# A sliding-window copy: the last staged batch shifted by one block and stored from 128 partitions, and fewer direct rows sent in halves

## Chip, core and metric

The kernel runs on one core of a Trainium2 chip. The metric is device time in microseconds (us), the median of several executions. The program does nothing but copy, so everything below is about the 16 DMA engines of the core, about HBM, the large memory of the chip, and about SBUF, the memory inside the core (128 rows, called partitions).

Two things about the numbers. First, times of one kernel on one chip agree within 1 per cent, mostly within 0.4, in four sets of experiments, each set on one chip. Here they are called chips A, B, C and D. (The chips of the very first runs, before and changed, are not on record.) Kernels are compared within one set only. Each chip was used in one set, so a lasting property of the chip and its condition at that hour (what else used its memory, for example, which is not on record) cannot be told apart; "chip" below means both. Second, all runs were of the fast state: every granted clock on record is 1.0.

## The reference

`x` has shape (32, 4096, 256), float32. Windows of 64 rows start every 32 rows; there are 127 in each of the 32 batches.

```python
for i in range(127):
    result[:, i] = x[:, 32 * i : 32 * i + 64].copy()
```

A *block* is 32 rows, 32 KB. A batch has 128 blocks. Window `w` is blocks `w` and `w + 1`: all blocks but the first and the last of a batch are written twice. The output is 266 MB.

## The kernel before

There are two ways to fill the output.

- **Direct**: HBM to HBM. One window (64 KB) is read and written, as two packets of 32 KB. A byte of output costs a byte of HBM reads and one pass through a DMA engine.
- **Staged**: a batch is loaded once into SBUF (128 partitions, one block each) and stored twice, as first halves and as second halves of the windows. It spares half of the reads, but three passes through the engines serve two bytes of output. Packets are 16 KB.

Eleven of the 32 batches are staged. Three of the core's engines issue the transfers: SP the direct windows (DMA queue q1), ACT the loads and stores (q10), and POOL the edge windows that are left over (q0), at the end. All three queues share the 16 engines. A direct transfer of 16 windows gives each engine two packets and one small completion packet. The same 16 windows "in halves" are two transfers, so each engine gets two packets and *two* completion packets. The kernel before uses that to set the balance of the queues.

```python
    def windows(self, q, b, w0, n, half=None, piece=DIRECT, count=None):
        size = 2 * blk if half is None else blk
        off = blk if half else 0
        # ... one DMA: n rows of `size`, x to out, step 2 * blk in out and blk in x

# Staging.store, the last staged batch (batch 30)
        if g == len(self.batches) - 1:
            for half, p0, rows in ((0, 0, 112), (0, 112, 15), (1, 1, 15), (1, 16, 112)):
                self.c.count_last(self.c.store(q, self.tiles[i], self.batches[g], half, p0, rows))
            return
        for half in (0, 1):    # all others: 128 partitions, one row too many each time
            self.c.store(q, self.tiles[i], self.batches[g], half).then_inc(self.stored[i], 16)

# the direct batches, seven groups of 16 windows each
    per, loads, stores = 6, 6 * 17, 34
                at = turns % (loads + per * stores)
                share += 9 if at < loads else 3      # twelfths: 3/4 in loads, 1/4 in stores
                if share >= 12:
                    share -= 12; turns += 4
                    c.windows(ring_d, b, first(b) + 16 * j, 16, 0)
                    c.windows(ring_d, b, first(b) + 16 * j, 16, 1, ...)
                else:
                    turns += 3
                    c.windows(ring_d, b, first(b) + 16 * j, 16, ...)
# ... the edge windows
        ring_r = nc.gpsimd
        ring_r.wait_ge(near, 16)                     # q1 is nearly done
        for i, b in enumerate(...):
            for g in waits[b]:
                st.wait_stored(ring_r, g)            # a staged store spilled one row here
            for w, n in rest_parts(b):
                c.windows(ring_r, b, w, n, None, PIECES[i % 1], count_soft)
```

A store of 128 rows for 127 windows writes one wrong row into a neighbouring batch. The edge windows there are copied after that store and put it right. The last staged batch, 30, has no such cover, so it is stored as 112 and 15 rows.

## Time and profile before

| | before |
|---|---|
| median time (first three runs) | 752.06 us |
| span of the profiled execution | 743.5 us |
| bytes through the engines | 313.16 MB |

These lines are from the profile page of the kernel before: the span; the DMA row (busy share of the engines in 40 slices, 9 is 90 per cent or more); the rate in the same slices; the queues with packets, MB and share of the engines' time.

```profile
span 743.5 us, 321 instructions
DMA  8999999999999999999999999999999999999995
GB/s 368 431 430 427 426 436 436 423 440 420 431 432 425 427 438 420 435 427 421 439 423 408 431 434 432 434 424 433 427 437 429 430 425 437 421 435 432 414 420 191
q1 hardware_dynamic: 8080, 154.15, 48.5%
q10 hardware_dynamic: 9002, 138.35, 43.8%
q0 software_dynamic: 1008, 20.65, 6.8%
```

The engines are busy from the second slice to the last but one. The kernel can get faster only by moving fewer bytes, by quicker packets, or by a better end.

The windows view shows stretches: start and end in us, length, POOL's busy time with instructions, tensor clock, busy share of the DMA engines, GB/s.

```profile
20.00:140.00 120.00, 0.00 (x0) 1.00 1.00 429
140.00:400.00 260.00, 0.00 (x0) 1.00 1.01 428
700.00:720.00 20.00, 0.00 (x0) 1.00 0.98 415
720.00:735.00 15.00, 0.00 (x0) 1.00 0.98 362
735.00:743.50 8.50, 0.00 (x0) 1.00 0.05 19
```

The rate is level until the end. From 720 us on, the engines are busy but slower. In the DMA view of 725 to 735 us (queues as above), hardly anything but edge windows is left:

```profile
q0 software_dynamic: 161, 3.24, 87.5%
q10 hardware_dynamic: 12, 0.11, 3.3%
```

In the packet records of the trace, a 16 KB packet takes 0.611 us and a 32 KB packet 1.213 us when nothing hinders it (these are the medians before). The **excess** is the time that packets take above this, summed and divided by 16 engines: microseconds of span lost to slow packets.

### The profile page before, as it was taken

Reading aid. Unit: us, or ns where it says so; the run is one execution under the profiler, and the core shown is the slowest. Engines: PE = TensorE matmul, PEld = TensorE weight load, DVE = VectorE, ACT = ScalarE, POOL = GpSimd, SP = SyncE. Lnnn points to the kernel's source line nnn. Section 1 sums busy time; section 2 is a strip of 40 time slices with the busy share of each in tenths; the row PEclk is TensorE's granted clock in tenths of the full one; section 3 lists DMA queues with packets and bytes.
Section 4 is the critical chain, followed back from the end, with each engine's and each line's share of the span. In section 5 each row is a group of like instructions: output and inputs, shape, how many; then the busy total and the mean of one; then the engine's idle time right before and its main releaser. Section 6 shows DMA issues by size and latency. Waiting matters only on the chain.

```text
span 743.5 us, 321 instructions
## 1 busy us (share of the span) xinstructions
POOL 12.4 (2%) x25
## 2 busy tenths in 40 slices
POOL 0000000000000000000000000000000000050000
DMA  8999999999999999999999999999999999999995
GB/s 368 431 430 427 426 436 436 423 440 420 431 432 425 427 438 420 435 427 421 439 423 408 431 434 432 434 424 433 427 437 429 430 425 437 421 435 432 414 420 191
DMA packets 18092, 313.16 MB, mean 421 GB/s; under 512 B 4312, under 2 KB 4312, under 8 KB 4312
## 3 DMA queue, kind: packets, MB, share of 16 engines
q1 hardware_dynamic: 8080, 154.15, 48.5%
q10 hardware_dynamic: 9002, 138.35, 43.8%
q0 software_dynamic: 1008, 20.65, 6.8%
q14 instruction: 2, 0.02, 0.0%
HBM read 220.92 MB, written 266.99 MB: 656 GB/s over the span
## 4 chain that ended last, share of the span: by engine, by line
another core or an unknown queue 91%; POOL 2%; issue 0%; POOLq 0%; SPq 0%
POOL out_dram L48 2%; POOLq L226 0%; SPq L165 0%; POOLq L107 0%
## 5 line engine op out<-in xcount | busy, mean ns | idle before, releaser
L48 POOL DMA_DIRECT2D out_dram<-in_x_dram x21 | 12.2, 584 | 674.3 <-DMA out_dram<-in_x_dram 651.4
L212 POOL MEMSET const-float32-0.0<- 128x1 f32 x1 | 0.1, 93 | 0.2 <-issue 0.2
L212 POOL MEMSET const-bfloat16-1.0<- 128x1 bf16 x1 | 0.1, 97 | 0.0
L212 POOL MEMSET const-uint8-127<- 128x1 uint8 x1 | 0.1, 93 | 0.0
L212 POOL MEMSET const-float32-1.0<- 128x1 f32 x1 | 0.1, 92 | 0.0
## 6 DMA issues: line engine op xcount, KB each, us to landing
out_dram<-in_x_dram SPq DMA_DIRECT2D x83, 1024.0 KB, 97.1
out_dram<-xb ACTq DMA_DIRECT2D x20, 4096.0 KB, 137.8
out_dram<-in_x_dram SPq DMA_DIRECT2D x128, 512.0 KB, 90.5
xb<-in_x_dram ACTq DMA_DIRECT2D x11, 4096.0 KB, 122.1
out_dram<-in_x_dram POOLq DMA_DIRECT2D x21, 960.0 KB, 46.5
out_dram<-xb ACTq DMA_DIRECT2D x2, 3584.0 KB, 127.3
out_dram<-xb ACTq DMA_DIRECT2D x2, 480.0 KB, 112.8
```

The costliest lines, as they stand in the source:

```text
L48: q.dma_start(out=self.oap((b * self.nw + w0) * 2 * blk + off, [[2 * blk, n], [1, size]]), in_=bass.AP(self.x.tensor, self.x.offset + (b * ...
L212: nc = _bacc.Bacc("TRN2", target_bir_lowering=False, num_devices=1)
```

## The change

Two parts with one intent: a better balanced end. Batch 31 is staged in place of 30, loaded from one block earlier, so that both its stores have 128 partitions. Their first rows fall into the last two windows of batch 30 and are wrong there. A small transfer, the *repair*, rewrites these two windows after the last staged store. And fewer rows go in halves: a half in load phases (before: three quarters), a sixth in store phases (before: a quarter).

```diff
-    staged = [*range(1, B - 3, 3), B - 2]
+    staged = [*range(1, B, 3)]
...
+    st = Staging(c, tc, pool, x.dtype, staged, 6, {B - 1})    # {B - 1}: shifted by 1
...
-            out=t[:, :], in_=self.xap(b * self.nb, [[self.blk, self.nb], [1, self.blk]]),
+            in_=self.xap(b * self.nb - shift, [[self.blk, self.nb], [1, self.blk]]),
...
-        w = b * self.nw + p0 - half
+        w = b * self.nw - half - shift
...
-            for half, p0, rows in ((0, 0, 112), (0, 112, 15), (1, 1, 15), (1, 16, 112)):
-                self.c.count_last(self.c.store(q, self.tiles[i], self.batches[g], half, p0, rows))
-            return
...
-                share += 9 if at < loads else 3
+                share += 6 if turns % (loads + per * stores) < loads else 2
...
+                if todo == 7:      # the one row of batch 31 that the shift leaves out
+                    count(c.windows(ring_d, B - 1, c.nw - 1, 1, 1, 2048), done)
...
+        st.wait_stored(ring_r, len(staged) - 1)
+        ap = [[c.blk // 4, 8], [c.blk, 2], [1, c.blk // 4]]
+        oap = [[c.blk // 4, 8], [2 * c.blk, 2], [1, c.blk // 4]]
+        count(                     # the repair
+            ring_r.dma_start(
+                out=c.oap((last * c.nw + c.nw - 2) * 2, oap), in_=c.xap(last * c.nb + c.nw - 2, ap)
+            ),
+            rest,
+        )
```

The cut leaves out bookkeeping: semaphores, and a slightly different order of the edge windows.

More of the change, by code (lines that the diff above doesn't have):

```diff
@@ L9, with __init__ @@
 DIRECT, IN, OUT = 32768, 16384, 16384
-PIECES = (32768,)
 class Copier:
-    def __init__(self, nc, tc, x, out, B, L, D, W, S, n_win):
+    def __init__(self, x, out, B, L, D, W, S, n_win):
         assert W == 2 * S and L % S == 0
-        self.nc, self.tc, self.x, self.out = nc, tc, x, out
+        self.x, self.out = x, out
         self.B = B
@@ L22, in __init__ @@
         self.nw = n_win
-        self.total = 0
-        self.done = tc.alloc_semaphore("done")
-        self.last = tc.alloc_semaphore("last")
-        self.last_total = 0
     def xap(self, block, dims):
         return bass.AP(self.x.tensor, self.x.offset + block * self.blk, dims)
-    def oap(self, elem, dims):
-        return bass.AP(self.out.tensor, self.out.offset + elem, dims)
-    def count(self, dma):
-        dma.then_inc(self.done, 16)
-        self.total += 16
-    def count_last(self, dma):
-        dma.then_inc(self.last, 16)
-        self.last_total += 16
@@ L42, in windows, with oap @@
-    def windows(self, q, b, w0, n, half=None, piece=DIRECT, count=None):
-        blk = self.blk
-        size = 2 * blk if half is None else blk
-        off = blk if half else 0
-        (count or self.count)(
-            q.dma_start(
-                out=self.oap((b * self.nw + w0) * 2 * blk + off, [[2 * blk, n], [1, size]]),
-                in_=bass.AP(
-                    self.x.tensor,
-                    self.x.offset + (b * self.nb + w0) * blk + off,
-                    [[blk, n], [1, size]],
-                ),
-                max_dma_last_dim=piece,
-            )
+    def oap(self, half_window, dims):
+        return bass.AP(self.out.tensor, self.out.offset + half_window * self.blk, dims)
@@ L57, in windows, with load @@
+    def windows(self, q, b, w0, n, half=None, piece=DIRECT):
+        blk = self.blk
+        row = [1, 2 * blk if half is None else blk]
+        h = half or 0
+        return q.dma_start(
+            out=self.oap((b * self.nw + w0) * 2 + h, [[2 * blk, n], row]),
+            in_=self.xap(b * self.nb + w0 + h, [[blk, n], row]),
+            max_dma_last_dim=piece,
         )
-    def load(self, q, t, b):
+    def load(self, q, t, b, shift):
         return q.dma_start(
-            out=t[:, :], in_=self.xap(b * self.nb, [[self.blk, self.nb], [1, self.blk]]),
+            out=t[:, :],
+            in_=self.xap(b * self.nb - shift, [[self.blk, self.nb], [1, self.blk]]),
@@ L62, in load, with store @@
             max_dma_last_dim=IN,
         )
-    def store(self, q, t, b, half, p0=0, n=None):
-        blk = self.blk
-        n = self.nb if n is None else n
-        w = b * self.nw + p0 - half
+    def store(self, q, t, b, half, shift):
+        w = b * self.nw - half - shift
         return q.dma_start(
-            out=self.oap(w * 2 * blk + half * blk, [[2 * blk, n], [1, blk]]),
-            in_=t[p0 : p0 + n, :],
+            out=self.oap(2 * w + half, [[2 * self.blk, self.nb], [1, self.blk]]),
+            in_=t[:, :],
@@ L79, with __init__, shift @@
 class Staging:
-    def __init__(self, c, pool, dtype, batches, bufs):
-        self.c, self.batches = c, batches
+    def __init__(self, c, tc, pool, dtype, batches, bufs, shifted):
+        self.c, self.batches, self.shifted = c, batches, shifted
         self.tiles = [pool.tile([128, c.blk], dtype, name=f"xb{i}") for i in range(bufs)]
-        self.loaded = [c.tc.alloc_semaphore(f"loaded{i}") for i in range(bufs)]
-        self.stored = [c.tc.alloc_semaphore(f"stored{i}") for i in range(bufs)]
+        self.loaded = [tc.alloc_semaphore(f"loaded{i}") for i in range(bufs)]
+        self.stored = [tc.alloc_semaphore(f"stored{i}") for i in range(bufs)]
+    def shift(self, g):
+        return 1 if self.batches[g] in self.shifted else 0
     def load(self, q, g):
@@ L91, in load @@
             q.wait_ge(self.stored[i], 32 * n)
-        self.c.load(q, self.tiles[i], self.batches[g]).then_inc(self.loaded[i], 16)
+        self.c.load(q, self.tiles[i], self.batches[g], self.shift(g)).then_inc(self.loaded[i], 16)
     def store(self, q, g):
@@ L96, in store @@
         q.wait_ge(self.loaded[i], 16 * (n + 1))
-        if g == len(self.batches) - 1:
-            for half, p0, rows in ((0, 0, 112), (0, 112, 15), (1, 1, 15), (1, 16, 112)):
-                self.c.count_last(self.c.store(q, self.tiles[i], self.batches[g], half, p0, rows))
-            return
         for half in (0, 1):
-            self.c.store(q, self.tiles[i], self.batches[g], half).then_inc(self.stored[i], 16)
+            self.c.store(q, self.tiles[i], self.batches[g], half, self.shift(g)).then_inc(self.stored[i], 16)
     def wait_stored(self, q, g):
@@ L132, with count @@
     assert out.shape == (B, n_win, W, D)
-    c = Copier(nc, tc, x, out, B, L, D, W, S, n_win)
-    staged = [*range(1, B - 3, 3), B - 2]
+    c = Copier(x, out, B, L, D, W, S, n_win)
+    staged = [*range(1, B, 3)]
     direct = [b for b in range(B) if b not in staged]
     pool = ctx.enter_context(tc.tile_pool(name="xb", bufs=1))
-    st = Staging(c, pool, x.dtype, staged, 6)
-    ring_d, ring_s = nc.sync, nc.scalar
-    spilled = staged[:-1]
-    waits = {b: [g for g, n in enumerate(spilled) if abs(n - b) == 1] for b in direct}
-    per, loads, stores = 6, 6 * 17, 34
-    def first(b):
-        return 0 if b - 1 not in spilled else 8 if len(waits[b]) == 2 else 15
-    def rest_parts(b):
-        if len(waits[b]) == 2:
-            return [(0, 8), (120, 7)]
-        return [(0 if b - 1 in spilled else 112, 15)]
-    soft = tc.alloc_semaphore("soft")
-    soft_total = 0
-    near = tc.alloc_semaphore("near")
-    def mark(dma):
-        dma.then_inc(near, 16)
-    def count_soft(dma):
-        nonlocal soft_total
-        dma.then_inc(soft, 16)
-        soft_total += 16
+    st = Staging(c, tc, pool, x.dtype, staged, 6, {B - 1})
+    ring_d, ring_s, ring_r = nc.sync, nc.scalar, nc.gpsimd
+    done = tc.alloc_semaphore("done")
+    near = tc.alloc_semaphore("near")
+    rest = tc.alloc_semaphore("rest")
+    total = {done: 0, near: 0, rest: 0}
+    def count(dma, sem):
+        dma.then_inc(sem, 16)
+        total[sem] += 16
+    per, loads, stores = 6, 6 * 17, 34
+    todo = 7 * len(direct)
+    turns = share = 0
     with tc.tile_critical():
         st.run(ring_s)
-        turns = share = 0
-        rests = []
-        todo = 7 * len(direct)
         for b in direct:
+            w = 15 if b - 1 in staged else 0
             for j in range(7):
-                at = turns % (loads + per * stores)
-                share += 9 if at < loads else 3
+                todo -= 1
+                sem = near if todo == 2 else done
+                share += 6 if turns % (loads + per * stores) < loads else 2
                 if share >= 12:
@@ L177 @@
                     turns += 4
-                    c.windows(ring_d, b, first(b) + 16 * j, 16, 0)
-                    c.windows(ring_d, b, first(b) + 16 * j, 16, 1, count=mark if todo == 3 else None)
+                    count(c.windows(ring_d, b, w, 16, 0), done)
+                    count(c.windows(ring_d, b, w, 16, 1), sem)
                 else:
                     turns += 3
-                    c.windows(ring_d, b, first(b) + 16 * j, 16, count=mark if todo == 3 else None)
-                todo -= 1
-            rests.append(b)
-        ring_r = nc.gpsimd
+                    count(c.windows(ring_d, b, w, 16), sem)
+                w += 16
+                if todo == 7:
+                    count(c.windows(ring_d, B - 1, c.nw - 1, 1, 1, 2048), done)
         ring_r.wait_ge(near, 16)
-        for i, b in enumerate(sorted(rests, key=lambda b: max(waits[b], default=0))):
-            for g in waits[b]:
-                st.wait_stored(ring_r, g)
-            for w, n in rest_parts(b):
-                c.windows(ring_r, b, w, n, None, PIECES[i % 1], count_soft)
-        ring_d.wait_ge(c.done, c.total)
-        ring_d.wait_ge(soft, soft_total)
-        ring_d.wait_ge(c.last, c.last_total)
+        pieces = (32768,)
+        last = B - 2
+        for i, b in enumerate([*direct[:-1], last]):
+            for g, n in enumerate(staged):
+                if abs(n - b) == 1 and b != last:
+                    st.wait_stored(ring_r, g)
+            w, n = (112, 13) if b == last else (0, 15) if b - 1 in staged else (112, 15)
+            count(c.windows(ring_r, b, w, n, None, pieces[i % len(pieces)]), rest)
+        st.wait_stored(ring_r, len(staged) - 1)
[7 more added lines that the diff above has]
+        )
+        for sem in (done, near, rest):
+            ring_d.wait_ge(sem, total[sem])
 _INS = ['x', 'window_size', 'stride']
```

## The prediction

> **What bounds the kernel now.** The 16 DMA engines. The DMA row of the page is 9 in 38 of 40 slices, and the windows view gives 427 to 433 GB/s in every stretch from 20 to 700 us. 313.16 MB pass the engines; at 429 GB/s that is 730 us of the 743.5 us span. The packet records show back-to-back packets: 16 KB takes 0.611 us, 32 KB 1.213 us. No compute engine matters (POOL 12.4 us busy).
>
> What is not at that rate is the end. The windows view: 700 to 720 us 415 GB/s, 720 to 735 us 362, 735 to 743.5 us 19. The DMA view of 725 to 735 us has q0 (the edge windows, HBM to HBM) at 87.5% of the engines and q10 (staging) at 3.3%; the 32 KB packets there take 1.4 to 1.5 us. The staging queue ends at 734.0 us, q0 at 740.1. The 5.6 MB moved after 720 us would take 13.0 us at 429 GB/s and took 20.1: about 7 us lost, partly because almost only direct copies are left, which read and write HBM (2 x 357 = 714 GB/s; the Trainium skill, HBM Reference, Specifications, gives about 716 for a domain; the trace agrees), partly because one engine ends 4 us after the rest.
>
> **What the change does.** Bytes hardly move: the shifted tile spills one block per store, as the other ten do, +0.065 MB = 0.15 us. Direct DMAs on q1 fall from 211 to 192, each 16 completion packets of 9 ns: 0.2 us. So there is no gain in the steady part; the change shifts the balance of the queues. Engines take turns between queues, so fewer halves (fewer completion packets) give q1 a larger share: counted in turns, q1 to q10 goes from 1.13 to 1.21 in loads and from 1.30 to 1.34 in stores (the DMA view of before shows 22.78 to 19.97 MB and 43.72 to 33.62 MB, 1.14 and 1.30). By these shares q1 ends at about 650 us instead of 661, with about 19 MB of staging left instead of 15. q0 then starts at about 645, runs at 250 GB/s, ends at about 728 (it waits for the last but one staged batch, at about 712, just before it would run dry), and staging ends last, with some 5 MB of stores from SBUF that write HBM only and should keep 430 GB/s.
>
> Gain: most of the 7 us, an estimated 5. Cost: the repair of the last two windows of batch 30 is issued only after the last staged store has landed: wake-up, issue (0.58 us as the others), an HBM round trip, 16 KB on each of 8 engines (about 0.6 us): estimated 3 to 4 us, wholly on the critical path. Also a larger direct share can slow packets a little more in the store phases (there 32 KB means 1.22 to 1.236 us against 1.213): up to 1 us.
>
> **Prediction.** 750.5 us, range 745 to 756; faster by over 2%: 0.02, within 2%: 0.96, slower by over 2%: 0.02. Span about 742.
>
> **What would show it.** DMA view: q1 over 54% of the moved bytes in load phases and 57% in stores; q1's last packet near 650; q0's last packet before q10's. Windows view: at least 415 GB/s from 700 us to within 6 us of the last staged store, then 3 to 4 us with almost no traffic. Chain of waits: ends with POOL's last DMA waiting for the last staged store.
>
> **What would make it wrong.** q0 could still end last, if its wait for the last but one staged batch starves it; then the 7 us stay. A single queue of stores may not hold 430 GB/s. The steady rate could move by 1% either way with the new mix: 7 us, more than the whole expected effect.

## The result

| | before | changed |
|---|---|---|
| median of 6 runs each, us | 752.27 | 756.81 |
| ratio of fast runs | 1 | 1.0057 (95% interval 1.0041 to 1.0073) |

A ratio is the mean time of one kernel's fast runs over that of the other's of the same rounds, so not quite the ratio of the medians. The changed kernel is slower by about 4.5 us. That is within 2 per cent, as predicted, but outside the range, and of the other sign.

From the page of the changed kernel: span, rate, queues, and the repair in the list of DMA issues (transfers, KB, us from issue to landing).

```profile
span 755.9 us, 301 instructions
GB/s 369 432 403 415 413 425 415 436 422 416 416 426 426 417 425 420 422 424 422 422 421 404 420 430 418 428 421 424 427 418 427 420 420 421 436 426 424 421 422 180
q1 hardware_dynamic: 7792, 154.19, 48.4%
q10 hardware_dynamic: 8976, 138.41, 44.0%
q0 software_dynamic: 1056, 20.65, 6.5%
out_dram<-in_x_dram POOLq DMA_DIRECT2D x1, 128.0 KB, 2.7
```

The windows view of the changed kernel:

```profile
20.00:140.00 120.00, 0.00 (x0) 1.00 1.00 418
140.00:400.00 260.00, 0.00 (x0) 1.00 1.00 422
700.00:720.00 20.00, 1.73 (x3) 1.00 1.00 420
720.00:735.00 15.00, 0.00 (x0) 1.00 1.01 428
735.00:745.00 10.00, 0.00 (x0) 1.00 0.89 380
745.00:755.90 10.90, 0.56 (x1) 1.00 0.12 44
```

The chain of waits ends with the repair (start, duration, what):

```profile
712.92 1.73 POOL out_dram L34 x3
714.64 35.24 another core or an unknown queue
749.88 0.28 issue
750.17 0.56 POOL out_dram L166
```

Between 720 and 735 us the rate is 428 GB/s, where it was 362. But everywhere before, it is 418 to 422 instead of 428 to 429, and the repair comes after everything else. Yet the two spans differ by 12.4 us where the timed runs differ by 4.5. Something in these two profiles is not comparable. The steady rate was therefore the first thing to test.

### The profile page after: what moved, and what is told of

It is laid out like the page before. It is cut to its first block, busy times and chain, and to the rows that moved or that the text cites. A ratio compares the mean times of both kernels' runs of the same rounds, so it can differ in the third digit from the quotient of the medians.

```text
span 755.9 us, 301 instructions
## 1 busy us (share of the span) xinstructions
POOL 13.0 (2%) x26
## 4 chain that ended last, share of the span: by engine, by line
another core or an unknown queue 97%; POOL 2%; issue 0%; POOLq 0%; SPq 0%
POOL out_dram L34 2%; POOL out_dram L166 0%; POOLq L203 0%; SPq L131 0%; POOLq L85 0%
```

## The experiments

### Two by two, on chip A

Theory S says that the new shares slow the steady part. Rival R says that the shares cost nothing, and that the new batch and its repair cost all. Four kernels ran in one set on one chip, with five rounds each: before, before with the new shares alone, changed with the old shares, changed.

```diff
 # e2_before_new_shares
-                share += 9 if at < loads else 3
+                share += 6 if at < loads else 2
 # e3_after_old_shares (in the changed kernel)
-                share += 6 if turns % ... < loads else 2
+                share += 9 if turns % ... < loads else 3
```

> The kernel before, unchanged: how far do two executions of the same program differ in their steady rate? Theory S (the new shares of halves slow the steady part): the profile shows again 427 to 433 GB/s between 20 and 700 us and a span near 743.5 us. Rival R (the first profile of before fell in an unusually quick execution; its span of 743.5 us does not fit the median time of 752 us): the profile shows a steady rate near 424 GB/s and a span near 750 us. Timed ratio to before 1.000 within 0.002 either way.

> The kernel before with only the shares changed (half of the direct rows in loads and a sixth in stores in halves). Theory S: most of the measured +4.5 us comes from the shares, so 1.004 to 1.010 times before, with a steady rate some 1 per cent lower than that of the unchanged kernel on the same chip and a shorter end. Rival R (the shares cost nothing, the new last batch with its repair at the end costs all): 0.994 to 1.001 times before.

> The changed kernel with the old shares (three quarters in loads, a quarter in stores). Theory S: about as fast as before, 0.998 to 1.003, steady rate as in the unchanged kernel. Rival R: 1.004 to 1.008 times before, as slow as the changed kernel.

> The changed kernel, unchanged, on the same chip as the three others: ratio 1.004 to 1.007 again by both theories. Theory S: steady rate below that of the unchanged before kernel in the same set by 1 per cent or more. Rival R: the same steady rate as before's within 0.3 per cent, and the difference lies wholly in the last 20 us: the last staged store ends late on a few engines and the repair follows it by 3 us.

| chip A | ratio to before (95% interval) | span | excess 20 to 635 us | excess after 710 | last data packet of q10 / q0 / repair |
|---|---|---|---|---|---|
| e1, before | 0.9983 (0.9964 to 1.0001) | 742.4 | 4.5 | 1.4 | 731.4 / 738.9 / none |
| e2, new shares alone | 0.9993 (0.9975 to 1.0010) | 743.2 | 7.0 | 1.1 | 739.8 / 731.3 / none |
| e3, new batch alone | 1.0004 (0.9987 to 1.0021) | 744.6 | 3.3 | 3.1 | 730.4 / 740.9 / 735.7 |
| e4, changed | 1.0038 (1.0021 to 1.0056) | 747.4 | 8.0 | 0.2 | 740.9 / 734.8 / 744.0 |

The windows view of the unchanged kernel (e1) on this chip, and then of the changed one (e4):

```profile
20.00:140.00 120.00, 0.00 (x0) 1.00 1.00 428
140.00:400.00 260.00, 0.00 (x0) 1.00 1.01 428
720.00:735.00 15.00, 0.00 (x0) 1.00 0.96 370
735.00:745.00 10.00, 0.00 (x0) 1.00 0.05 23
```

```profile
20.00:140.00 120.00, 0.00 (x0) 1.00 1.00 424
140.00:400.00 260.00, 0.00 (x0) 1.00 1.01 426
720.00:735.00 15.00, 0.00 (x0) 1.00 0.99 422
735.00:745.00 10.00, 0.56 (x1) 1.00 0.24 95
```

On one chip the steady rate falls from 428 to 424 and 426, not to 418 and 422: much of the gap between the first two profiles was probably not the change. R's guess was that the first profile was a lucky execution. It is no longer needed: all runs on chip A are near 745 us, so there are *chips* on which the first profile's 743.5 us is ordinary.

Neither theory came out as put. The time of e2 lies in R's band and that of e3 in S's: on this chip each part alone is within noise of free, and only both together cost 0.4 per cent. S's mechanism is there, 2.5 to 3.5 us of excess with the new shares, but e2's end gives it back. The last column suggests why the parts do not add. With the old shares the edge windows (q0) end last, and the repair runs while they do. With the new shares staging (q10) ends last, and the repair stands alone behind it. This became the third theory.

### Is it the direct share, or the rows in halves? On chip B

Why are packets slower with the new shares? Theory D: a direct byte is read from and written to HBM, so a larger direct share of the bytes brings HBM nearer its limit. Rival H: rows in halves are quick for a reason of their own. The third kernel separates them: it sends rows in halves, but 32 windows to a transfer, so that each engine again gets two packets to one completion packet.

```diff
 # e5_no_halves                       # e6_all_halves
-  share += 9 if at < loads else 3    -  share += 9 if at < loads else 3
+  share += 0                         +  share += 12
 # e7_halves_of_32
+            c.windows(ring_d, b, first(b), 16)
+            for j in range(3):
+                at32 = first(b) + 16 + 32 * j
+                c.windows(ring_d, b, at32, 32, 0)
+                c.windows(ring_d, b, at32, 32, 1, ...)
```

> The kernel before with no direct rows in halves. Counted in turns, direct copies get 58.7 per cent of the bytes in loads and stores alike. Theory D (packets slow down as the direct share of the bytes rises, because a direct byte is read from and written to HBM): the excess of packet time over 0.611 and 1.213 us, summed over the packets up to q1's end and divided by 16 engines, was 4.7 us in the kernel before and 7.2 us with the new shares; here 10 to 15 us, and q1 ends near 630 us. Rival H (it is the rows in halves that are quick, whatever the share): also high here, 10 or more. Time 1.002 to 1.012 times before by both.

> Six of seven direct windows in halves, but 32 windows to a transfer, so that each engine still gets two packets of 32 KB to one completion packet: the direct share is 58.7 per cent, as with no halves, while nearly all rows are in halves. This tells the two apart. Theory D: excess up to q1's end as in the run without halves, within 3 us, 9 or more. Rival H: excess 5 us or less. Time: D 1.002 to 1.012, H 0.992 to 1.000 times before.

> The kernel before with all direct rows in halves, 16 windows to a transfer: direct share 51.5 per cent throughout. Theory D and rival H both: excess up to q10's end below 3.5 us. But staging then ends early (near 670 us) and what is left, some 28 MB of direct copies, runs alone at about 357 GB/s: total 1.010 to 1.025 times before. A steady excess as large as before's 4.7 us would speak against D.

> The kernel before, unchanged, for its profile on the chip of this set: the excess against which the other three are read. If this chip is the one of the first set: 4 to 5 us up to q1's end, span 742 to 745 us. If it is one of the slow kind (median 752 us): by theory D alone nothing is said; the excess should then be 10 to 13 us, since the bytes and the end are the same and only packet time can differ.

The DMA view from 160 to 390 us, queue by queue (packets, MB, share of the engines), first all halves (e6):

```profile
q1 hardware_dynamic: 3113, 51.09, 52.0%
q10 hardware_dynamic: 3105, 47.73, 48.6%
```

Before (e9):

```profile
q1 hardware_dynamic: 2741, 55.22, 56.9%
q10 hardware_dynamic: 2741, 42.29, 43.6%
```

No halves (e5):

```profile
q1 hardware_dynamic: 2578, 56.33, 59.1%
q10 hardware_dynamic: 2580, 39.68, 41.5%
```

Halves of 32 (e7):

```profile
q1 hardware_dynamic: 2590, 56.66, 59.0%
q10 hardware_dynamic: 2590, 39.81, 41.5%
```

The two queues send the same *number* of packets, to within 8 of 3,100, whatever the sizes. That is what engines would do that alternate packet by packet, with a completion packet using up a turn. The Trainium skill, "DMA: Bandwidth & Descriptors", section "Queues, rings and completion order", says that each engine goes round robin between the queues at packet granularity. The counts agree if every record, even a 9 ns completion, is taken as a packet; the records do not name the engine, so the alternation itself was not seen. So the direct share of the bytes follows from the number of completion packets.

The rates in the same stretch, in the windows view, in the same order (e6, e9, e5, e7):

```profile
160.00:390.00 230.00, 0.00 (x0) 1.00 1.01 430
```

```profile
160.00:390.00 230.00, 0.00 (x0) 1.00 1.01 424
```

```profile
160.00:390.00 230.00, 0.00 (x0) 1.00 1.01 417
```

```profile
160.00:390.00 230.00, 0.00 (x0) 1.00 1.00 419
```

| chip B | direct share of bytes, 160 to 390 us | excess 20 to 635 us | ratio to before |
|---|---|---|---|
| e6, all halves | 0.517 | 1.8 | 1.0141 |
| e9, before | 0.566 | 9.7 | 1.0002 |
| e7, halves of 32 | 0.587 | 20.3 | 1.0244 |
| e5, no halves | 0.587 | 23.5 | 1.0277 |

D's order holds. The excess follows the direct share and is steep: seven points of share make more than 20 us. Six of seven rows in halves at the same share save 3.1 us up to q1's end, just over the 3 that D allowed, so H explains a small part at most. The *sizes* that I expected were wrong: I had 10 to 15 us for e5 and at most 1.012 for e5 and e7, and below 3.5 us up to q10's end for e6, which has about 4 from 20 us on. The same table tells what the excess of the kernel before is on this chip: 9.7 us against 4.5 on chip A. In all it is 14.5 against 7.7 us, and the spans, 749.2 against 742.4, differ by the same 6.8 us. **The difference between these two executions is packet time alone.**

In the steady part of these four kernels a larger share goes with fewer completion packets (0.39 for each data packet in e6, 0.25 in e5), so these runs alone do not tell the two apart. The end of e6 does. There direct copies run alone (all of q0), with 0.59 completions for each data packet, and their 32 KB packets are the slowest of the set (a mean of 1.59 us, against 1.26 in e5 from 160 to 390 us). The windows view of that stretch:

```profile
695.00:740.00 45.00, 5.51 (x10) 1.00 1.00 328
```

How near is the limit? An estimate: at a rate `r` with a direct share `d`, HBM reads and writes together are r x (1 + d). At the unhindered 430 GB/s that would be 652, 673 and 682 GB/s for 0.517, 0.566 and 0.587. At the measured rates it is 652 (e6), 664 (e9), 662 (e5) and 665 (e7), and 2 x 328 = 656 with direct copies alone. So on this chip the kernels that ask for more than about 665 GB/s do not get it, while e6, which asks for 652, is hardly slowed. That is what a ceiling of HBM would look like, and it supports D; what sets it (reads and writes together, their mixture, the addresses) was not tried. The rate that is reached differs from chip to chip: on chip A the steady part of e1 moved 429 x 1.568 = 673 GB/s with 4.5 us of excess, and the first profile of before had 2 x 357 = 714 GB/s at its end, as the prediction read it from the records.

e6 shows the other side: its steady part is nearly perfect, but staging ends at 669 us and some 86 us of direct copies alone follow. It is 1.4 per cent slower. e5 was worse than its steady part explains. There, with staging alone on the engines, its last stores slowed down. From 730 us on, by the bytes left (8.0 MB), these are the 112 and 15 rows of the old batch form, which hold 8.3 MB; just before, they are mostly rows of 128. The windows view of e5, with all engines busy and no packets of q0 or q1:

```profile
724.00:727.00 3.00, 0.00 (x0) 1.00 1.01 431
730.00:739.00 9.00, 1.15 (x2) 1.00 1.00 306
```

The 16 KB packets took 0.61 us in the first stretch and 0.84 to 0.86 in the second.

### The repair and the two shares, on chip C

The repair is taken out of the changed kernel (two windows are then wrong; the program still waits for the last stores). Two more kernels have the new share in one kind of phase only.

```diff
 # e8_no_repair (in the changed kernel)
-        st.wait_stored(ring_r, len(staged) - 1)
-        ... the repair
+        st.wait_stored(ring_d, len(staged) - 1)
 # e10: "9 if at < loads else 2"; e12: "6 if at < loads else 3" (in the kernel before)
```

> The changed kernel once more, as the measure for the run without the repair: 1.003 to 1.007 times before; in its profile the repair's packets end 2.9 to 3.3 us after the last packet of the staging queue and are the last data packets of the program.

> The changed kernel without the repair of the last two windows of batch 30 (these two windows are wrong on purpose); the program still waits for the last staged stores. If the repair lies wholly on the critical path: 2.5 to 3.5 us below the changed kernel of the same set, so 0.999 to 1.003 times before. If it is hidden (another transfer ends later anyway): no change, within 1 us.

> The kernel before with the new share in store phases only (a sixth), three quarters in loads as before. The profiles so far put the larger part of the added packet time into load phases (0.8 to 1.7 and 0.04 to 1.0 us per 100 us, against 0.8 to 1.0 in stores), and this edit moves q1's end by about 4 us, which should let staging and the edge windows end together, near 735 us instead of 733 and 739. Theory: 0.996 to 1.000 times before, at most 1 us more excess, 2 us less loss at the end. If the end does not get shorter, 1.000 to 1.003.

> The kernel before with the new share in load phases only (a half), a quarter in stores as before. Theory: excess up to q1's end rises by 1.5 to 3 us over the kernel before on the same chip, nearly all in the load phases and there in the 16 KB packets; the end becomes about 2 us shorter; 0.999 to 1.004 times before, slower than the run with the new share in stores only by 1 to 3 us. If both runs are alike, the phase does not matter and only the mean share does.

| chip C | median us | ratio to before (95% interval) |
|---|---|---|
| before | 752.89 | 1 |
| e11, changed | 756.72 | 1.0056 (1.0034 to 1.0078) |
| e8, changed without the repair | 753.59 | 1.0008 (0.9989 to 1.0027) |
| e10, new share in stores only | 753.56 | 1.0005 (0.9985 to 1.0024) |
| e12, new share in loads only | 753.56 | 1.0006 (0.9985 to 1.0026) |

The repair costs 3.1 us of time (every run of e11 is slower than every run of e8), and without it the changed kernel is as fast as before within noise. In e11's records the last packet of q10 ends at 748.2 us and the repair's at 751.4.

e10 is a miss. Its end was as balanced as I wanted, 746.4 and 747.0 us for q10 and q0, but the gain I expected did not come, and e12 has the same median. That load phases matter more than store phases is not confirmed. No profile of before was taken on this chip, so the excess there (12.7 us in e10 and 13.3 in e12 from 20 to 635 us) has nothing to be held against.

### The four again, on chip D

> The kernel before, unchanged: ratio 1.000 within 0.002. On a slow chip (median 750 us and up) the excess of packet time up to q1's end is 9 to 13 us; on a quick one (745 us) 4 to 5. Edge windows end last, 5 to 7 us after the staging queue.

> The changed kernel: 1.003 to 1.007 times before. Excess up to q1's end 2.5 to 5 us above that of before on the same chip (if it is equal, the gap between the first two profiles was the chip alone). Staging ends after the edge windows, the repair 3 us after that, last of all.

> Before with the new shares only: 0.998 to 1.002 times before. Excess as in the changed kernel within 1.5 us; staging ends last; the loss at the end about 2 us below before's.

> The changed kernel with the old shares: 0.999 to 1.002 times before. Excess as in before within 1.5 us; the repair is issued before the edge windows end, so it is hidden and the edge windows end last.

| chip D | ratio to before (95% interval) | span | excess 20 to 635 us | excess after 710 | last data packet of q10 / q0 / repair |
|---|---|---|---|---|---|
| e13, before | 1.0003 (0.9988 to 1.0018) | 744.3 | 4.7 | 2.0 | 733.5 / 740.8 / none |
| e15, new shares alone | 1.0022 (1.0007 to 1.0037) | 746.6 | 8.5 | 1.4 | 743.2 / 732.7 / none |
| e16, new batch alone | 1.0015 (1.0000 to 1.0030) | 746.0 | 6.2 | 2.5 | 731.4 / 742.3 / 738.5 |
| e14, changed | 1.0039 (1.0022 to 1.0056) | 748.2 | 8.5 | 0.1 | 741.6 / 735.5 / 744.8 |

POOL's issue of the repair in the timeline (start, us, and in brackets the wait before it), first e14 and then e16:

```profile
742.31 0.56 POOL L166 DMA_DIRECT2D out_dram<-in_x_dram  x1 [36.79 <-DMA out_dram<-xb]
```

```profile
733.08 0.56 POOL L166 DMA_DIRECT2D out_dram<-in_x_dram  x1 [44.24 <-DMA out_dram<-xb]
```

In e14 the repair is issued after all other data has landed, in e16 nine microseconds before the last edge window ends. So the order of the ends, and with it the exposure of the repair, repeated. That the parts do not add did not clearly repeat: on chip D the two parts alone cost 0.22 and 0.15 per cent and both together 0.39, which is their sum within noise. The excess in the steady part rose by 3.8 us with the whole change (3.5 on chip A). e15's time is a little over its band, and e16's excess is more above before's than I allowed: two profiles with the same shares differ by up to 1.5 us there (4.7 and 6.2 here), so a single difference of that size means nothing.

One benefit of the new batch form also shows. With the new shares and the *old* form, the last stores ran at a mean of 0.69 us for each 16 KB from 733 us on (e15); with the new form it is 0.611 (e14). That is the excess after 710 us: 1.4 against 0.1 here, 1.1 against 0.2 on chip A. The records tell more when they are sorted by the staged bytes that are left. The two 15-row stores of the old form begin with 4.65 MB left. Between 4.9 and 4.2 MB, the 16 KB packets of the six old-form kernels on chips A, C and D take 0.67 to 0.81 us, and those of the six new-form kernels 0.61 to 0.65. On chip B, with staging alone on the engines, it is 1.32 us (e5) and 1.25 (e7); there the 112 rows before them are slow too, as shown above. The very last stores are not always slow: in e12, which has the old form, they ran at 0.611 us from 733 us on. So the 15-row stores are the likelier cost. Why is open, and no run changed that form alone.

## Why the prediction was wrong

- **What bounds the kernel: right.** The engines are busy throughout, and the bytes did not matter.
- **"No gain in the steady part", with "up to 1 us" for slower packets: this step failed, together with the next.** The direction was named, the size was missed: 3.5 to 3.8 us came in place of 1. (The prediction did list, as what would make it wrong, that the steady rate could move by 1 per cent, 7 us, but its sum did not allow for it.) The excess from 20 to 635 us rose by 3.5 us (chip A) and 3.8 us (chip D). I had read 1.22 to 1.236 us against 1.213 for the direct packets in the store phases and took it for a detail. It was the foot of a steep curve, as the experiments on chip B showed.
- **"Gain: an estimated 5": too large, 1.5 to 3.7 in its place.** On chip A this step missed by at least as much as the one above, on chip D by less. Less excess after 710 us gave 1.2 us on chip A and 1.9 on chip D. The span without all excess and without the repair (3.1 and 3.2 us from q10's last packet to the repair's) is shorter by 0.3 and 1.8 us. Together 1.5 to 3.7 us. Direct copies alone at the end did go, but staging ends ragged too: in e14 the engines moved 141 GB/s on average from 735 to 745 us.
- **The repair, "3 to 4 us, wholly on the critical path": right.** 3.1 us of time, by e8 against e11.
- **The shift of the queues: right in kind.** Staging ends after the edge windows, and q1, completions included, ended 7 us earlier (chips A and D), where I said 11. The last edge windows were released by the last but one staged batch at 704 us on chip D and 713 in the first profile, where I said 712, and did not run dry.
- **The sum.** Predicted: -5 at the end, +3 to 4 for the repair, up to +1 for slow packets. Measured in the profiles: -1.5, +3.1 and +3.5 on chip A, where the span rose by 5.0 us; -3.7, +3.2 and +3.8 on chip D, where it rose by 3.9, of which another 0.7 lies in slow packets of the first 20 us. The part of the gain that is not excess is what was left over, so these sums close by construction; the excess and the repair are measured. In the timed runs the loss was 0.38 to 0.57 per cent, 3.2 to 4.5 us, in all four sets that held the changed kernel.
- **A reading error ahead of all that.** The profile on which I costed everything gave 743.5 us, and 745.3 as its own time, while the timed median was 752. I took the gap for overhead of timing. It was most likely another, quicker chip (its chip is not on record): span and time of the same execution differ by less than 2 us, and its excess of 7.8 us is that of the quick chips A and D (7.7 and 8.3). So I took an excess of 4.1 us for the steady part that would have been near 10 on a chip like B. There it would have been plain that packet time is the term that varies.

What stays open: why chips differ in packet time, or in the HBM rate that they reach; why the 15-row stores of the old form are slow; and how the shares alone split on a slow chip, where no profile of before and of the changed kernel stand side by side. No version tried beats the kernel before. With 735 us of e1's span free of excess, set by its bytes, its start and its end, little is left to win: at most its 7.7 us of excess, 1 per cent, and a little at the end (an estimate).

## What to carry to other kernels

When all DMA engines are busy, look at how long a packet takes, not only at whether the engines are busy: a mix that reads and writes HBM more can lose several microseconds at 100 per cent busy (23.5 against 9.7 us of excess in e5 and e9). Completion packets count as turns of their queue, so the number of transfers shifts the balance between queues (direct shares of 0.517 to 0.587 here), and a change of balance decides which queue ends last; a small dependent transfer is hidden behind one ending and costs its whole latency behind the other. And check that the profile and the timed runs agree before costing a change from it: if they do not, they may come from different chips.

## What the Trainium skill lacked or had wrong

- HBM Reference, section "Specifications", gives about 716 GB/s for a domain. The end of the first profile of before agrees (2 x 357 = 714 GB/s with direct copies nearly alone). It does not say that what one core reaches can differ from chip to chip: on chip B direct copies alone moved 2 x 328 = 656 GB/s for 45 us with all engines busy, and three kernels stayed at 662 to 665 by the estimate above. Whether the other core of the domain was idle is not on record.
- DMA: Bandwidth & Descriptors, section "Queues, rings and completion order", gives a packet as typically 9 to 17 descriptors. Here two queues matched each other in the number of records (2,741 and 2,741 in 230 us), completions of 9 ns included, though q1 has a completion after every one or two data records and q10 after every eight. The page does not say that completions use up turns.
- The same page, section "Rules for kernel authors", asks for 128 partitions. What fewer cost stands elsewhere, in SBUF — State Buffer, section "Door 1", by the number of ports that a range of partitions reaches, but with no rate for 112 rows or for several such stores in flight together. Here, stores of 112 and 15 rows ran at 306 GB/s with all engines busy, where mostly rows of 128 just before ran at 431 (the cause is open; no run tests the ports).
- DMA: Bandwidth & Descriptors, section "Anatomy of one DMA — SWDGE (gpsimd) path", gives about 2.0 us plus bytes over 436 GB/s, an estimate of 2.3 us for the 128 KB repair. With nothing else on the engines the runs show 2.7 to 2.9 us from issue to landing, and 3.1 of time.
- No page says that the same program can differ between chips: medians of 745.6 to 752.9 us, and in one profile each on two of them 6.8 us of span, all of it packet time.
